# A decoder step on one core: half of the recurrence's tables on VectorE, and the sampled scores spread for two sequences at once

## The chip, the core and the metric

The kernel runs on one core of a Trainium2 chip, as one program. The metric is the device time of one execution in microseconds (us); less is better. TensorE (PE) multiplies matrices, VectorE (DVE) and GpSimd (POOL) work elementwise, ScalarE (ACT) copies and evaluates functions, and SyncE (SP) issues every DMA of this kernel, one after another. Each engine executes its own instructions in the order in which they stand in its queue.

## The reference, cut to what matters

One layer of a hybrid decoder for a prompt of 1024 rows and for 8 sequences of 8 new rows (64 sampled rows). One input projection gives queries, keys, values and the input u of a state-space group.

```
z = rmsnorm(x) @ w_in                      # 1088 rows, 1024 -> 2048 columns: q, k, v, u
# window attention, three dilations (1, 4, 16), for prompt and sample
scores = einsum(q, k) / 8 ;  p = softmax ;  out = p @ v
# S5 recurrence: h[t] = a*h[t-1] + B u[t] ;  y[t] = Re(C h[t]) + D u[t]    (complex, 32 groups x 64 states)
y = x + concat(norm(attn), norm(ssm)) @ w_out ;  y = y + (silu(y@w_gate) * (y@w_up)) @ w_down
```

For the sample, each query meets a cache of 2048 past keys per sequence: every 16th key of the far part (96 per query row), every 4th of the middle part, and all of the last 128. The recurrence is computed in blocks of 8 time steps: an input table (B times the powers of a, per group) takes 8 inputs to a state, and an output table (C times the powers of a) takes a state to 8 outputs.

## The kernel before

The program has three stages, and the change lies in the first.

**Stage A (the input projection, to about 315 us of the span).** TensorE computes 16 column pieces of `w_in` by 1088 rows; pieces 0 to 3 are q, 4 to 7 are k, 8 to 11 are u, 12 to 15 are v. Every number is split into two parts, so each product is three matmuls (lines 70, 71, 72). A piece needs its weights split: `ws`, high part by ScalarE (line 64), low part by VectorE (line 65). A k piece is copied out by ScalarE (`kr`, `kh`) and by VectorE (`kl`, line 65), and only then is its PSUM bank free for the piece three further on. Banks of tag `sd` serve the work beside the projection.

Two generators run beside the projection, and `merge` decides by their yielded weights which one writes its next instructions; a scheduler then orders each engine's queue by a timeline of its own.

- `ssm_setup` and `ssm_units`: a long chain of small VectorE instructions (`pw`, `wph`, then `D1`/`D2`, the input factors), then for 8 units `products(u)` on GpSimd: the input table `vt` (lines 574 to 576 from `D1`, `D2`) and the output table `WO` (the same three lines from `E1`, `E2`), both 128x512. `vt` and `WO` have two buffers each. `turn(u)` transposes `vt` on TensorE, `shift(q)` multiplies by `shf`, and `tables()` makes the rotation table `CP` on VectorE (lines 618 to 620). The results go to DRAM.
- `sample_scores`: 24 steps, three for each sequence. A step loads far keys `kf` and middle keys `kk`, multiplies them with the queries `qb` (`kf` on GpSimd, line 679; `kk` on VectorE, line 680), and sums over 64 columns (`Sm`, line 687; `Sf`, line 689 by VectorE or line 694 by ScalarE). After two sequences, `rest(g)` spreads the sums against selection matrices (`Z`, line 722; `Y`, line 725) and TensorE gathers them with 12 small matmuls (`sel,Z` and `sel,Y`, line 75).

**Stage B (315 to 660 us)**: prompt attention, the recurrence itself and the sampled values; it starts with loads of the stored queries and keys (`QS`, `KH`, `KL`). **Stage C (from 660 us)**: output projection and FFN.

Of the kernel before, what the change touches and what calls it, by code (L numbers as in the profile page):

```python
# [46 lines left out]
class K:  # L47
# [506 lines left out]
    def ssm_units(self, wk):  # L554
# [6 lines left out]
        def products(u):  # L561
            gs = slice(4 * u, 4 * u + 4)

            def pwb(z):
                return z[:, :, gs].rearrange("p k g -> p g k").unsqueeze(2).to_broadcast(shp)

            def mb(m):
                return m[:, gs].unsqueeze(3).to_broadcast(shp)
            wo = wk.tile([128, 4, 128], F32, tag="WO", name="WO", bufs=2)
            vt[u] = wk.tile([128, 4, 16, 8], F32, tag="vt", name="vt", bufs=2)  # L570
            ca = wo.rearrange("p g (c d) -> p g c d", c=16)
            for o, m1, m2, z in ((vt[u], D1, D2, pwr), (ca, E1, E2, pw[:, :, 1:9])):
                o2 = wk.tile([128, 4, 16, 8], F32, tag="v2", name="v2", bufs=1)
                G.tensor_tensor(out=o, in0=mb(m1), in1=pwb(z[:, 0]), op=OP.mult)
                G.tensor_tensor(out=o2, in0=mb(m2), in1=pwb(z[:, 1]), op=OP.mult)
                G.tensor_tensor(out=o, in0=o, in1=o2, op=OP.add)
            self.store(self.dWO[u], wo)

        def turn(u):
# [12 lines left out]
            V.tensor_copy(k, p[:, 0:64].rearrange("p (g c) -> p g c", c=16))  # L592
            V.tensor_tensor(k, k, dd[:, 4 * u:4 * u + 4], op=OP.add)
# [54 lines left out]
    def sample_scores(self, sp, sq):  # L648
# [3 lines left out]
        kf, kk, qb, kn, kt, Sf, Sm = ({} for _ in range(7))  # L652
        sel = sp.tile([128, 68], F32, name="sel")
        self.load(sel, I["c_sel"])
        tsel, asel, bsel, xsel = sel[:, 0:8], sel[:, 12:28], sel[:, 28:60], sel[:, 60:68]


        def loads(i):
# [15 lines left out]
            kk[i] = sq.tile([128, 3, 512], F32, tag="kk", name="kk", bufs=KKB)  # L674
            self.load(kk[i][:, 0], ck[b, 1536 + 128 * u:1664 + 128 * u])

        def products(i):
            b, u = divmod(i, 3)
            nc.gpsimd.tensor_tensor(out=kf[i], in0=kf[i], in1=qb[b][:, 0:1].to_broadcast((128, 2, 512)), op=OP.mult)  # L679
            V.tensor_tensor(out=kk[i][:, 1:3], in0=kk[i][:, 0:1].to_broadcast((128, 2, 512)), in1=qb[b], op=OP.mult)  # L680

        def reduce(i):
            b, u = divmod(i, 3)
            if u == 0:
                Sf[b] = sp.tile([128, 6, 8], F32, tag="Sf", name="Sf", bufs=3)
                Sm[b] = sp.tile([128, 3, 2, 8], F32, tag="Sm", name="Sm", bufs=3)
            V.tensor_reduce(Sm[b][:, u], kk[i][:, 1:3].rearrange("p j (h e) -> p j h e", e=64), axis=AX.X, op=OP.add)
# [30 lines left out]
        def rest(g):  # L718
            Z = sp.tile([128, 6, 2, 8, 8], F32, tag="Z", name="Z", bufs=1)
            Y = sp.tile([128, 2, 3, 2, 8, 8], F32, tag="Y", name="Y", bufs=1)  # L720
            for a in range(2):
                V.tensor_tensor(Z[:, :, a], Sf[2 * g + a].unsqueeze(3).to_broadcast((128, 6, 8, 8)),
                                tsel.unsqueeze(1).unsqueeze(1).to_broadcast((128, 6, 8, 8)), op=OP.mult)
                for v in range(2):
                    V.tensor_tensor(Y[:, v, :, a], Sm[2 * g + a][:, :, v].unsqueeze(3).to_broadcast((128, 3, 8, 8)),
                                    (tsel, xsel)[v].unsqueeze(1).unsqueeze(1).to_broadcast((128, 3, 8, 8)), op=OP.mult)
            p = self.bank("sd")
            for j in range(6):
                self.mm1(p[:, 16 * j:16 * j + 16], Z[:, j].rearrange("p a h t -> p (a h t)"), asel)
            for j in range(3):  # L730
                for v in range(2):
                    self.mm1(p[:, 96 + 32 * j:128 + 32 * j], Y[:, v, j].rearrange("p a h t -> p (a h t)"), bsel, v == 0, v == 1)
            nc.scalar.activation(self.S[:, g, 0:192], p[:, 0:192], AF.Copy)

        nc.gpsimd.memset(self.S[:, :, 320:384], 0.0)
        loads(0)
        for i in range(25):
            b, u = divmod(i, 3)
            loads(i + 1)
            if i < 24:  # L740
# [7 lines left out]
            elif u == 1 and b % 2 == 0 and b > 0:  # L748
                rest(b // 2 - 1)
            yield 4.2  # L750
        self.scores_end = (lambda: near(7), lambda: rest(3))


    def sample_values(self, sp):
# [31 lines left out]
        def soft3(g):  # L786
# [6 lines left out]
                            sel[:, 8:12].unsqueeze(1).to_broadcast((128, 96, 4)), op=OP.mult)  # L793
# [1169 lines left out]
def consts():  # L1963
# [21 lines left out]
    for b in range(8):  # L1985
# [7 lines left out]
    d["c_sel"] = np.concatenate([r[:, None] % 8 == np.arange(8), r[:, None] % 4 == np.arange(4),  # L1993
                                 r[:, None] // 8 == np.arange(16), r[:, None] // 4 == np.arange(32), (r[:, None] + 4) % 8 == np.arange(8)], axis=1).astype(np.float32)
# [27 lines left out]
```

## Time and profile before

| | |
|---|---|
| median of 3 runs | 1549.76 us (1548.33 to 1554.3) |
| the profiled execution, its own time | 1551.42 us |
| span in the profile | 1549.3 us |
| busy PE, DVE, ACT, POOL | 94%, 70%, 46%, 48% of the span |
| mean granted TensorE clock | 0.933 of full speed |

The shares are averages over the three stages. In stage C TensorE is nearly always busy; the places where TensorE stands idle or at half its clock lie in stages A and B. The rows further down are therefore taken from stretches of stage A.

### The profile page before, as it was taken

The page shows a single profiled execution, that of the slowest core. Times are in us where ns is not written, and L with a number is a line of the kernel's source. Part 1 is how long each engine was busy: PE and PEld are TensorE (multiplying, and loading weights), DVE is VectorE, ACT ScalarE, POOL GpSimd, SP SyncE. Part 2 cuts the span into 40 slices and gives each one's busy share as a digit, 9 for nine tenths or more (in the row PEclk, how much of TensorE's full clock was granted, in tenths as well). Part 3 has the DMA queues.
Part 4 walks back from the last instruction along what each step waited for, and adds up shares of the span by engine and source line. Part 5 has one row for each costly group of instructions (what it writes and reads, how often), then busy time and mean ns, then how long its engine had stood idle before and what let it go on. Part 6 is the DMA issues. An engine that isn't in the chain of part 4 may idle for free.

```text
span 1549.3 us, 28207 instructions
## 1 busy us (share of the span) xinstructions
PE 1449.9 (94%) x10005; PEld 1350.3 (87%) x10005; DVE 1078.1 (70%) x2226; ACT 716.6 (46%) x1815; POOL 744.5 (48%) x719
## 2 busy tenths in 40 slices
PE   6988988989899999899987999999999989999996
PEld 5988978867777667699987999999999989999996
DVE  7895399858856677687989555555555577579554
ACT  6233444345467667665453333333322364466443
POOL 3059545436735454411147678788775421114331
PEclk9998988958769999889998999999999999999998
DMA  9438887797775863443342266566564368689874
GB/s 222 159 115 295 246 243 231 220 240 185 198 184 159 202 168 89 141 147 119 109 127 82 92 205 217 180 198 206 176 205 135 107 252 297 191 297 329 234 233 127
DMA packets 244187, 292.90 MB, mean 189 GB/s; under 512 B 29870, under 2 KB 185358, under 8 KB 244046
## 3 DMA queue, kind: packets, MB, share of 16 engines
q1 hardware_dynamic: 244046, 291.10, 62.8%
q8 instruction: 79, 1.29, 0.4%
q14 instruction: 62, 0.51, 0.1%
HBM read 211.69 MB, written 79.35 MB: 188 GB/s over the span
## 4 chain that ended last, share of the span: by engine, by line
PE 67%; DVE 14%; DMA 8%; issue 4%; POOL 3%; ACT 2%; SPq 2%; POOLq 0%; DVEq 0%; ACTq 0%
PE pmm L70 16%; PE pmm L72 16%; PE pmm L71 16%; PE psd L75 7%; PE pmm L75 3%; PE ptr L79 2%; PE ppo L75 2%; DMA kk<-in_cache_attn_k_dram 1%; SPq L82 1%; DVE ws L65 1%; POOL P L1176 1%; PE ptr L75 1%; DMA hs<-dH 1%; DVE kk L680 1%; DMA wr<-in_w_in_dram 1%
## 5 line engine op out<-in xcount | busy, mean ns | idle before, releaser
L70 PE MATMUL pmm<-hn,ws 128*128 128x272 f32 x1232 | 358.9, 291 | 9.7 <-DVE u L1750 4.4
L72 PE MATMUL pmm<-hn,ws 128*128 128x272 f32 x1232 | 357.4, 291 | 1.9 <-DVE ws L65 1.9
L71 PE MATMUL pmm<-hn,ws 128*128 128x272 f32 x1232 | 356.4, 290 | 1.0 <-DVE hn L65 1.0
L64 ACT ACTIVATE ws<-wr 128x512 fp32r<-128x512 f32 (+2 forms) x238 | 151.6, 644 | 206.1 <-PE pmm L72 192.2
L70 PEld LDWEIGHTS pmm<-hn,ws 128*128 128x128 f32 x1232 | 233.5, 190 | 11.5 <-DVE u L1750 4.7
L72 PEld LDWEIGHTS pmm<-hn,ws 128*128 128x128 f32 x1232 | 233.1, 189 | 2.5 <-DVE ws L65 2.3
L71 PEld LDWEIGHTS pmm<-hn,ws 128*128 128x128 f32 x1232 | 233.4, 190 | 1.7 <-DVE hn L65 1.6
L65 DVE TENSOR_TENSOR ws<-wr,ws 128x512 fp32r<-128x512 f32 (+2 forms) x238 | 200.4, 848 | 48.1 <-ACT ws L64 46.7
L70 PE MATMUL pmm<-hs,ws 128*128 128x272 f32 x448 | 131.3, 294 | 5.0 <-ACT hs L64 5.0
L72 PE MATMUL pmm<-hs,ws 128*128 128x272 f32 x448 | 131.0, 295 | 0.4 <-DVE ws L65 0.4
L71 PE MATMUL pmm<-hs,ws 128*128 128x272 f32 x448 | 131.1, 293 | 0.0
L1754 POOL TENSOR_TENSOR hid<-hid,s 128x272 f32<-128x272 f32 x88 | 82.3, 941 | 55.6 <-DVE hid L1747 55.6
L65 DVE TENSOR_TENSOR ws<-st,ws 128x512 fp32r<-128x512 f32 x72 | 61.1, 850 | 59.2 <-ACT ws L64 59.2
L826 POOL TENSOR_TENSOR vs<-vr,vs 128x512 fp32r<-128x512 f32 x40 | 56.2, 1410 | 94.6 <-ACT vs L824 82.0
L679 POOL TENSOR_TENSOR kf<-kf,qb 128x1024 f32<-128x1024 f32 x24 | 63.9, 2672 | 63.2 <-DMA kf<-in_cache_attn_k_dram 30.8
L70 PEld LDWEIGHTS pmm<-hs,ws 128*128 128x128 f32 x448 | 85.8, 192 | 5.2 <-ACT hs L64 5.2
L72 PEld LDWEIGHTS pmm<-hs,ws 128*128 128x128 f32 x448 | 85.3, 191 | 0.8 <-DVE ws L65 0.7
L71 PEld LDWEIGHTS pmm<-hs,ws 128*128 128x128 f32 x448 | 85.9, 192 | 0.0
L1123 DVE CUSTOM_DVE_ANT_0 P<-pmm,lnc 128x256 f32<-128x256 f32 (+1 forms) x128 | 47.6, 377 | 54.8 <-PE pmm L75 43.4
L64 ACT ACTIVATE ws<-st 128x512 fp32r<-128x512 f32 x72 | 45.2, 628 | 80.7 <-PE pmm L72 69.3
L70 PE MATMUL pmm<-mT,ws 128*128 128x272 f32 x256 | 75.6, 300 | 0.0
L71 PE MATMUL pmm<-mT,ws 128*128 128x272 f32 x256 | 75.5, 298 | 0.0
(441 smaller groups left out, 4106.0 us busy)
## 6 DMA issues: line engine op xcount, KB each, us to landing
vr<-in_cache_attn_v_dram SPq DMA_DIRECT2D x80, 256.0 KB
wr<-dS SPq DMA_DIRECT2D x32, 512.0 KB
hs<-dH SPq DMA_DIRECT2D x28, 544.0 KB
kf<-in_cache_attn_k_dram SPq DMA_DIRECT2D x48, 256.0 KB
wr<-in_ffn_w_gate_dram SPq DMA_DIRECT2D x24, 512.0 KB
wr<-in_ffn_w_up_dram SPq DMA_DIRECT2D x24, 512.0 KB
wx<-dS SPq DMA_DIRECT2D x24, 512.0 KB
dH<-hid SPq DMA_DIRECT2D x22, 544.0 KB
```

The source lines that it names most:

```text
L64: self.nc.scalar.activation(hi, src, AF.Copy)
L65: (eng or self.nc.vector).tensor_tensor(out=lo, in0=src, in1=raw(hi), op=OP.subtract)
L70: nc.tensor.matmul(out, lhsT=wh, rhs=xh, start=start, stop=False)
L71: nc.tensor.matmul(out, lhsT=wh, rhs=xl, start=False, stop=False)
L72: nc.tensor.matmul(out, lhsT=wl, rhs=xh, start=False, stop=stop)
L75: self.nc.tensor.matmul(out, lhsT=w, rhs=x, start=start, stop=stop)
L79: self.nc.tensor.transpose(out, in_, self.ident[:n, :n])
L82: return self.nc.sync.dma_start(out=out, in_=in_).ins
L679: nc.gpsimd.tensor_tensor(out=kf[i], in0=kf[i], in1=qb[b][:, 0:1].to_broadcast((128, 2, 512)), op=OP.mult)
L826: eng.tensor_tensor(out=s[:, 1], in0=vr[i], in1=raw(s[:, 0]), op=OP.subtract)
L1123: V.tensor_tensor_reduce(out=P[h, g].rearrange("p b k -> p (b k)")[:, o:o + n], in0=s[:, o:o + n], in1=lnc[:, part, 256 - n:256], scale=-1 ...
L1754: self.mark = G.tensor_tensor(out=o, in0=o, in1=sb, op=OP.mult).ins
```

## The change: what it does

1. `products(u)`: the input table `vt` stays on GpSimd, the output table `WO` is now made by VectorE, and each has its own helper tile (`v0`, `v1`).
2. `turn(u)`: two VectorE instructions for `kr` (a copy out of PSUM, then an addition of `dd`) become one that adds while it reads PSUM.
3. `ssm_units`: the rotation table advances twice in each unit, between yields of 6.0, instead of once (four times in unit 0) between yields of 3.5.
4. `sample_scores`: the raw middle keys have their own tile `kr` with three buffers, loaded two steps ahead (`mids`), instead of a third of the tile `kk`, which was loaded one step ahead and had two buffers. `Sf` and `Sm` hold two sequences. `rest` becomes `rest1` (one `Z` and one `Y` of 128x768 each for both sequences, where 2 of 128x384 and 4 of 128x192 stood) and, one step later, `rest2` with the matmuls. A step yields 3.6 instead of 4.2. The columns of the constant `c_sel` are put in another order.

```diff
-            for o, m1, m2, z in ((vt[u], D1, D2, pwr), (ca, E1, E2, pw[:, :, 1:9])):
-                o2 = wk.tile([128, 4, 16, 8], F32, tag="v2", name="v2", bufs=1)
-                G.tensor_tensor(out=o, in0=mb(m1), in1=pwb(z[:, 0]), op=OP.mult)
...
+            for k, (eng, o, m1, m2, z) in enumerate(((G, vt[u], D1, D2, pwr), (V, ca, E1, E2, pw[:, :, 1:9]))):
+                o2 = wk.tile([128, 4, 16, 8], F32, tag=f"v{k}", name="v2", bufs=1)
+                eng.tensor_tensor(out=o, in0=mb(m1), in1=pwb(z[:, 0]), op=OP.mult)
+                eng.tensor_tensor(out=o2, in0=mb(m2), in1=pwb(z[:, 1]), op=OP.mult)
+                eng.tensor_tensor(out=o, in0=o, in1=o2, op=OP.add)
...
-            V.tensor_copy(k, p[:, 0:64].rearrange("p (g c) -> p g c", c=16))
-            V.tensor_tensor(k, k, dd[:, 4 * u:4 * u + 4], op=OP.add)
+            V.tensor_tensor(k, p[:, 0:64].rearrange("p (g c) -> p g c", c=16), dd[:, 4 * u:4 * u + 4], op=OP.add)
...
-            yield 3.5
-            for _ in range(4 if u == 0 else 1):
+            for _ in range(2):
                 next(tab, None)
-            yield 3.5
+                yield 6.0
...
+        def mids(i):
+            if i < 24:
+                b, u = divmod(i, 3)
+                kr[i] = sq.tile([128, 512], F32, tag="kr", name="kr", bufs=3)
+                self.load(kr[i], ck[b, 1536 + 128 * u:1664 + 128 * u])
...
+        def rest1(g):
+            Z[g] = sp.tile([128, 6, 128], F32, tag="Z", name="Z", bufs=1)
+            Y[g] = sp.tile([128, 2, 3, 128], F32, tag="Y", name="Y", bufs=1)
...
             loads(i + 1)
+            mids(i + 2)
...
             elif u == 1 and b % 2 == 0 and b > 0:
-                rest(b // 2 - 1)
-            yield 4.2
-        self.scores_end = (lambda: near(7), lambda: rest(3))
+                rest1(b // 2 - 1)
+            if u == 2 and b % 2 == 0 and b > 0:
+                rest2(b // 2 - 1)
+            yield 3.6
+        self.scores_end = (lambda: near(7), lambda: rest1(3), lambda: rest2(3))
```

The queues change as follows. In VectorE's queue of before, where the phases `wph` of the rotation are squared and renormalised (between the outputs `ql` of the last q piece), the chain stands by itself:

```order
L479 TENSOR_SCALAR t_672<-t_672 128x32
L480 TENSOR_TENSOR wph<-wph,t_672 128x32
L481 TENSOR_TENSOR wph<-wph,t_672 128x32
L450 TENSOR_TENSOR t_672<-wph 128x32
L451 TENSOR_TENSOR t_673<-wph 128x32
L452 TENSOR_TENSOR t_674<-wph 128x32
L453 TENSOR_TENSOR t_675<-wph 128x32
```

At the same place VectorE's queue now holds the output tables `WO` of the units between the links of that chain (`v` is their helper tile):

```order
L577 TENSOR_TENSOR WO<-WO,v_1079 128x512
L478 TENSOR_TENSOR t_672<-t_672,t_673 128x32
L575 TENSOR_TENSOR WO<-E_164,pw 128x512
L576 TENSOR_TENSOR v_1187<-E_165,pw 128x512
L479 TENSOR_SCALAR t_672<-t_672 128x32
L260 SCALAR_TENSOR_TENSOR ql<-pmm,qh 128x384
L577 TENSOR_TENSOR WO<-WO,v_1187 128x512
L480 TENSOR_TENSOR wph<-wph,t_672 128x32
L481 TENSOR_TENSOR wph<-wph,t_672 128x32
```

All 24 instructions of `WO` moved ahead of the instructions that finish `D1` and `D2`, on which GpSimd's input tables wait.

In TensorE's queue of before, the matmuls on the first `Z` stand in the middle of the last u piece (bank `ppo`), and those on `Y` 18 projection matmuls later:

```order
L72 MATMUL ppo<-xT_118,ws 128x448
L75 MATMUL psd<-sel,Z 128x16 x6
L79 MATMUL psd<-ident,kn 128x128 x4
L70 MATMUL ppo<-xT_118,ws 128x448
L71 MATMUL ppo<-xT_118,ws 128x448
```

Now they stand together, in the v pieces:

```order
L72 MATMUL pmm<-ws,xT_116 128x256
L79 MATMUL psd<-ident,kn 128x128 x4
L75 MATMUL psd<-sel,Z 128x16 x6
L75 MATMUL psd<-sel,Y 128x32 x6
L70 MATMUL ppo<-ws,xT_117 128x256
```

The first `Z` moved behind 66 more projection matmuls. The second one moved from 1008 to 1200 of the 1296 projection matmuls; the third and fourth stand behind the last one, as before.

In VectorE's queue of before, around the first `Z` and `Y`, the two halves of `Z` are apart (`QB` is another operand of TensorE, `kk`, `Sm`, `Sf` the products and sums):

```order
L680 TENSOR_TENSOR kk<-kk,qb 128x1024
L722 TENSOR_TENSOR Z<-Sf,sel 128x6x64
L687 TENSOR_REDUCE Sm<-kk 128x16
L689 TENSOR_REDUCE Sf<-kf 128x16
L680 TENSOR_TENSOR kk<-kk,qb 128x1024
L725 TENSOR_TENSOR Y<-Sm,sel 128x3x64 x2
```

Now:

```order
L693 TENSOR_REDUCE Sm<-kk 128x2x8 x2
L729 TENSOR_TENSOR Y<-Sm,sel 128x768
L684 TENSOR_TENSOR kk<-kr,qb 128x1024 x2
L693 TENSOR_REDUCE Sm<-kk 128x2x8
L695 TENSOR_REDUCE Sf<-kf 128x2x8
L693 TENSOR_REDUCE Sm<-kk 128x2x8
L695 TENSOR_REDUCE Sf<-kf 128x2x8
L713 COPY QB_101<-QR 64x4x8 x2
L727 TENSOR_TENSOR Z<-Sf,sel 128x768
```

One `Y` and one `Z` stand where six instructions stood; ahead of the `Z` there are now 9 products and 14 sums of the scores, where 6 and 9 stood.

## Rows read from the trace of the kernel before

**Rows 1.** Windows: stretch, its length, busy us (instructions) by engine, clock, DMA share, GB/s.

```profile
60.00:100.00 40.00, 40.00 (x252) 38.39 (x251) 38.97 (x163) 10.88 (x28) 13.24 (x10) 1.00 0.45 144
100.00:126.00 26.00, 14.64 (x89) 13.25 (x88) 25.83 (x25) 7.13 (x13) 21.92 (x12) 0.82 0.32 112
126.00:186.00 60.00, 60.00 (x391) 58.10 (x391) 20.48 (x26) 24.48 (x45) 40.19 (x29) 0.96 0.88 292
186.00:315.00 129.00, 111.52 (x808) 106.90 (x806) 111.81 (x104) 51.19 (x313) 63.67 (x27) 0.88 0.83 234
315.00:660.00 345.00, 324.21 (x1476) 247.15 (x1475) 246.30 (x685) 210.02 (x577) 175.96 (x245) 0.83 0.66 174
```

**Rows 2.** Windows: the three stretches of stage A at half the clock.

```profile
215.80:226.00 10.20, 6.96 (x26) 6.58 (x27) 8.64 (x12) 1.96 (x17) 4.12 (x2) 0.50 0.88 265
253.30:263.50 10.20, 6.95 (x32) 6.95 (x33) 8.60 (x11) 2.16 (x15) 5.29 (x2) 0.50 0.81 254
116.80:130.40 13.60, 7.84 (x31) 7.76 (x32) 13.57 (x10) 4.75 (x10) 13.37 (x8) 0.50 0.53 191
```

**Rows 3.** Timeline of PE: start, us, instruction [idle before it <- releaser].

```profile
115.31 0.44 PE L70 MATMUL pmm<-xT,ws 128*128 128x384 f32 x1 [3.77 <-DVE kl L65]
...
219.03 2.31 PE L75 MATMUL psd<-sel,Z 128*128 128x16 f32 x10 [5.61 <-DVE Z L722]
...
256.55 0.64 PE L75 MATMUL psd<-sel,Y 128*128 128x32 f32 x2 [4.82 <-DVE Y L725]
```

**Rows 4.** Timeline of DVE, 86 to 101 us: one form alone and beside GpSimd.

```profile
86.05 0.20 DVE L619 TENSOR_TENSOR CP<-CP,wpk 128x64 f32<-128x64 f32 x1
...
86.92 0.67 DVE L524 TENSOR_TENSOR D<-D,u 128x512 f32<-128x512 f32 x1
...
89.04 1.41 DVE L619 TENSOR_TENSOR CP<-CP,wpk 128x64 f32<-128x64 f32 x1
```

**Rows 5.** Timeline of POOL: the first input table, and one beside VectorE.

```profile
87.67 2.70 POOL L574 TENSOR_TENSOR vt<-D,pwr 128x512 f32<-128x512 f32 x2 [18.34 <-DVE D L524]
...
115.97 2.24 POOL L576 TENSOR_TENSOR vt<-vt,v 128x512 f32<-128x512 f32 x1
```

**Rows 6.** Groups by line, POOL, 60 to 180 us: count, busy us, mean ns.

```profile
L575 POOL TENSOR_TENSOR v<-E,pw 128x512 f32<-128x512 f32 x8 | 13.3, 1668 | 0.4
...
L574 POOL TENSOR_TENSOR WO<-E,pw 128x512 f32<-128x512 f32 x8 | 12.6, 1578 | 29.7 <-DVE t L479 24.3 <-DMA dWO<-WO 5.4
```

**Rows 7.** Groups by line and form, DVE, 60 to 180 us.

```profile
L593 DVE TENSOR_TENSOR kr<-kr,dd 128x64 f32<-128x64 f32 x8 | 9.3, 1158 | 0.2
...
L592 DVE COPY kr<-psd 128x64 f32<-128x64 f32 x8 | 1.7, 218 | 7.1 <-PE psd L75 7.1
```

**Rows 8.** Groups by line, DVE, 180 to 310 us.

```profile
L680 DVE TENSOR_TENSOR kk<-kk,qb 128x1024 f32<-128x1024 f32 x24 | 39.9, 1670 | 22.5 <-DMA kk<-in_cache_attn_k_dram 22.5
L687 DVE TENSOR_REDUCE Sm<-kk 128x16 f32<-128x1024 f32 x24 | 28.9, 1210 | 0.3
...
L725 DVE TENSOR_TENSOR Y<-Sm,sel 128x192 f32<-128x192 f32 x16 | 9.7, 650 | 0.0
...
L722 DVE TENSOR_TENSOR Z<-Sf,sel 128x384 f32<-128x384 f32 x8 | 4.4, 558 | 0.2
```

**Rows 9.** Timeline of DVE: first product, last spread, first instruction of prompt attention.

```profile
186.28 2.83 DVE L680 TENSOR_TENSOR kk<-kk,qb 128x1024 f32<-128x1024 f32 x1 [17.38 <-DMA kk<-in_cache_attn_k_dram]
...
307.10 1.16 DVE L725 TENSOR_TENSOR Y<-Sm,sel 128x192 f32<-128x192 f32 x4
...
315.09 0.29 DVE L1123 CUSTOM_DVE_ANT_0 P<-pmm,lnc 128x128 f32<-128x128 f32 x1 [6.83 <-PE pmm L75]
```

**Rows 10.** Chain that ended last, in order of time: start, us, what.

```profile
172.24 1.78 PE psd L75 x16
...
302.08 0.39 ACT vr L365
...
307.55 6.98 DMA KL<-dK
```

More of the change, by code (lines that the diff above doesn't have):

```diff
@@ L651, in sample_scores @@
         ck = I["cache_attn_k"][0].rearrange("b p h e -> b p (h e)")
-        kf, kk, qb, kn, kt, Sf, Sm = ({} for _ in range(7))
+        kf, kr, kk, qb, kn, kt, Sf, Sm, Z, Y = ({} for _ in range(10))
         sel = sp.tile([128, 68], F32, name="sel")
         self.load(sel, I["c_sel"])
-        tsel, asel, bsel, xsel = sel[:, 0:8], sel[:, 12:28], sel[:, 28:60], sel[:, 60:68]
+        tsel, txsel, asel, bsel = sel[:, 0:8], sel[:, 0:16].rearrange("p (v t) -> p v t", v=2), sel[:, 20:36], sel[:, 36:68]
         def loads(i):
@@ L679, in products @@
             nc.gpsimd.tensor_tensor(out=kf[i], in0=kf[i], in1=qb[b][:, 0:1].to_broadcast((128, 2, 512)), op=OP.mult)
-            V.tensor_tensor(out=kk[i][:, 1:3], in0=kk[i][:, 0:1].to_broadcast((128, 2, 512)), in1=qb[b], op=OP.mult)
+            kk[i] = sq.tile([128, 2, 512], F32, tag="kk", name="kk", bufs=KKB)
+            V.tensor_tensor(out=kk[i], in0=kr[i].unsqueeze(1).to_broadcast((128, 2, 512)), in1=qb[b], op=OP.mult)
         def reduce(i):
             b, u = divmod(i, 3)
[L684 to L687, printed above, removed]
+            g, a = divmod(b, 2)
+            if u == 0 and a == 0:
+                Sf[g] = sp.tile([128, 6, 2, 8], F32, tag="Sf", name="Sf", bufs=2)
+                Sm[g] = sp.tile([128, 2, 3, 2, 8], F32, tag="Sm", name="Sm", bufs=2)
+            V.tensor_reduce(Sm[g][:, :, u, a], kk[i].rearrange("p j (h e) -> p j h e", e=64), axis=AX.X, op=OP.add)
             if u != 1:
-                V.tensor_reduce(Sf[b][:, 2 * u:2 * u + 2], kf[i].rearrange("p j (h e) -> p j h e", e=64), axis=AX.X, op=OP.add)
+                V.tensor_reduce(Sf[g][:, 2 * u:2 * u + 2, a], kf[i].rearrange("p j (h e) -> p j h e", e=64), axis=AX.X, op=OP.add)
                 return
@@ L693, in reduce @@
                     x = kf[i][:, j, 64 * h:64 * h + 64]
-                    nc.scalar.activation(x, x, AF.Copy, accum_out=Sf[b][:, 2 + j, h:h + 1])
+                    nc.scalar.activation(x, x, AF.Copy, accum_out=Sf[g][:, 2 + j, a, h:h + 1])
         def turn(b):
@@ L792, in soft3 @@
             V.tensor_tensor(Z[:, 768:1152].rearrange("p (a t) -> p a t", t=4), S[:, g, 96:192].unsqueeze(2).to_broadcast((128, 96, 4)),
-                            sel[:, 8:12].unsqueeze(1).to_broadcast((128, 96, 4)), op=OP.mult)
+                            sel[:, 16:20].unsqueeze(1).to_broadcast((128, 96, 4)), op=OP.mult)
             for j0, n in ((0, 4), (4, 4), (8, 2)):
@@ L1991, in consts @@
     d["c_csel"] = (r[:, None] % 64 == np.arange(64)[None, :]).astype(np.float32)
-    d["c_sel"] = np.concatenate([r[:, None] % 8 == np.arange(8), r[:, None] % 4 == np.arange(4),
-                                 r[:, None] // 8 == np.arange(16), r[:, None] // 4 == np.arange(32), (r[:, None] + 4) % 8 == np.arange(8)], axis=1).astype(np.float32)
+    d["c_sel"] = np.concatenate([r[:, None] % 8 == np.arange(8), (r[:, None] + 4) % 8 == np.arange(8), r[:, None] % 4 == np.arange(4),
+                                 r[:, None] // 8 == np.arange(16), r[:, None] // 4 == np.arange(32)], axis=1).astype(np.float32)
     return d
```

24 lines of the change are left out of this document (9 added, 15 removed).

## The prediction

> **What bounds the kernel now.** I began with the windows of busy time, cut where the work changes. The changed code runs from about 60 to 310 us. From 60 to 100 us TensorE never pauses while VectorE is busy 38.97 of 40 us; from 100 to 126 TensorE works only 14.64 of 26 us and VectorE 25.83; from 126 to 186 TensorE is full again and VectorE has 40 us to spare; from 186 to 315 TensorE lacks 17.5 us and VectorE is busy 111.81 of 129 [rows 1]. So the set-up of the recurrence is held by VectorE, the middle by TensorE, and the scores by VectorE with TensorE waiting on it.
>
> TensorE's timeline names the waits to be seen in the two thin stretches: 3.77 us for `kl` at 115, 5.61 us for the first `Z`, 4.82 us for a `Y` [rows 3]. After such holes the granted clock stood at half, 1.2 GHz, three times in stage A: 116.8 to 130.4, 215.8 to 226.0 and 253.3 to 263.5 us [rows 2]. Work at half clock takes twice its time, so the loss is half the busy time there: 3.9, 3.5 and 3.5 us. Where the chain leaves stage A, it goes from the last v piece's copy at 302.08 through SP's queue to the load of `KL`, 6.98 us [rows 10], and prompt attention's first VectorE instruction comes at 315.09, 13.0 us behind that copy; VectorE's last spread had ended at 307.10 + 1.16 = 308.26 [rows 9]. TensorE's chain is thus the later one, by 6.8 us.
>
> **The change part by part.**
>
> *Output tables on VectorE.* GpSimd loses 24 instructions, three groups of 8 at 1668 to 1578 ns, about 38.5 us [rows 6]. VectorE gets 24 of 128x512. The nearest row, an addition of this size with two SBUF inputs, took 0.67 us [rows 4]: 24 x 0.67 = 16.1 us. I take that; the upper bound is GpSimd's own 1.6 us (38 us), should the powers' strided reading be slow there. In the order of VectorE's queue all 24 stand before `D1` and `D2` are finished, in the stretch where VectorE had 1 us to spare. Hence the first input table, which GpSimd began at 87.67 us behind `D` [rows 5], begins some 16 us later, near 104. Two buffers of `WO` put a wait for its store on VectorE, with `ql` and `kl` behind it; in the order 9 to 15 rows lie between a table's last addition and its buffer's next use, some 3 to 5 us, and I price the waits at 0 to 3 us.
>
> Then 24 GpSimd instructions of `vt` follow instead of 48. Alone one took 2.70 / 2 = 1.35 us, beside VectorE 2.24 [rows 5]; 24 of them are 32 to 54 us, so the last table is ready at 136 to 158, plus what the two `vt` buffers wait for TensorE. VectorE meets them with the same rotation table `CP`. A `CP` instruction of 128x64 took 0.20 us alone and 1.41 beside GpSimd [rows 4]: it ended with the GpSimd instruction. The joined `kr` should go the other way: with both inputs in SBUF the addition took 1158 ns, the copy from PSUM 218 [rows 7]; one instruction at 0.22 saves 8 x (1.158 + 0.218 - 0.22) = 9.2 us of VectorE, bounds 0 and 11.
>
> The Trainium skill, "SBUF — State Buffer", section "Who interferes with whom", says that a VectorE instruction with two SBUF inputs and a GpSimd instruction reading SBUF shut each other out for a whole instruction. The trace agrees (0.20 against 1.41). It speaks against a division of labour between these two engines: side by side, 24 + 24 would add up, 24 x 1.35 + 24 x 0.67 = 48 us. Here the order keeps `WO` out of the way, and the rule bears on `CP` alone. By it the joined `kr`, with one input in PSUM, is spared, which is the 9.2 us; without it the saving would be 8 x 0.218 = 1.7 us.
>
> For TensorE the two sides nearly balance. It gains from the projection's `kl` standing ahead of the large `CP` steps. It loses as `ws` and `kl` of the next k pieces stand among contended instructions, and as the transposes of units 0 to 6 now lie within 27 thousand projection columns, where they had been spread over 73 thousand: GpSimd, at 4 to 7 us a unit, can't keep up. I take 4 us later at the end of the k pieces, with 8 earlier and 10 later as bounds: the holes of before were at most some 11 us with 3.9 of clock.
>
> *The start of the scores.* The last `shf` matmuls, 172.24 us [rows 10], free the memory that the scores take over, and they stand in TensorE's order at nearly the same projection column as before, in a stretch without a hole. Finishing the tables sooner therefore brings nothing here. The raw keys' first load, now ahead of the queries' in SP's queue, does: the first product waited for its keys to 186.28 [rows 9]. I take 2 us (0 to 4).
>
> *Spreading for two sequences.* `Y` cost VectorE 9.7 us and `Z` 4.4 [rows 8]. Eight instructions of 768 elements, between the forms of 384 (558 ns) and 1024 (1670 ns with its share of contention), at 0.93 us are 7.4 us: 6.7 less. Three buffers of raw keys and a load two steps ahead take away the later waits for keys, 22.5 [rows 8] - 17.38 [rows 9] = 5.1 us; I count 3, since other waits take their place. VectorE then ends at 308.3 - 2 - 6.7 - 3 = 296.6, were TensorE not later.
>
> *TensorE's two holes.* The first `Z` stands 66 projection matmuls later; at 391 matmuls in 60 us [rows 1] that is 10 us. Against it, VectorE needs before it 9 products (1670), 14 sums (1210), two `ws` and four `QB` (together about 6 us), `Y` and `Z`: 15.0 + 16.9 + 6 + 1.9 = 39.8 us from the first product at about 184.3, so 224.1. TensorE, which waited from 219.03 - 5.61 = 213.4 [rows 3], would now arrive at 223.4. Of the hole about 1 us is left; with an error in it I count 2. The second `Z` stands 192 matmuls later, and VectorE has more than 10 us in hand there, so 4.82 us go. With the holes the two half-clock tails go, 3.5 + 3.5. Sum: 5.6 + 4.8 + 7.0 - 2 = 15.4 us.
>
> *Moved loads and shorter yields* change no amount of work; I price them at 0, with 3 us either way, because stores of v rows stand in SP's queue among loads that wait for VectorE.
>
> *The later stages.* The order in stage B is shuffled by some twenty places at most, with its middle unmoved; in the FFN it is the same word for word. Stage B has its own holes (324.21 busy of 345 us, clock 0.83 [rows 1]); 2% of it, 7 us either way, is what I grant to chance.
>
> **The sum.** TensorE: 302.1 + 4 - 15.4 = 290.7; plus 13.0 is 303.7. VectorE: 296.6 + 4 = 300.6, earlier, so it doesn't decide. Prompt attention begins 315.1 - 303.7 = 11.4 us sooner. The profiled execution took 1551.4, 1.7 over the median shown: 1540 against it and 1538 against the median. I say **1539 us**.
>
> **The rivals.**
>
> *The gain stops at the next late thing.* If VectorE's scores keep their 122 us from first product to last spread (contention moves from `Y` to the products) and the start slips by 4, VectorE ends at about 310, and with its own 13 us lead gone to nothing attention starts at 312 to 316: 0 to 3 us, about 1549. For it: VectorE is busy 87% there. Against: 16 small spreads less.
>
> *VectorE starves TensorE in the set-up (slower).* If an output-table instruction costs 1.4 us or more on VectorE, `D` comes 34 us later instead of 16, at about 121; 24 `vt` at 2.24 run to 175, and the last turn, shift and score loads come 14 us after today's; TensorE has its holes of 100 to 126 again behind it and half the clock. Even with 5 us won in the scores it ends near 1562. It decides from `D` ready later than about 115 us. For it: VectorE is full there. Against: 0.67 us for the nearest row.
>
> *Both thin stretches go.* If the projection also loses its 11 us of holes and 3.9 of clock, with VectorE at 296 or sooner, the time is about 1522. For it: `kl` stands sooner in the order. Against: the crowded turns.
>
> *The spread still holds TensorE* (the change doesn't do what it says): `Z` comes a hole later, nothing but the clock moves; 1548, within the first rival.
>
> **How the numbers follow.** The forecast has 0.52, its own range 1529 to 1547; the first rival 0.27 (1544 to 1556); the slower one 0.12; both stretches 0.09. A change under 0.5%, 7.7 us, can't be told from none with this kernel: faster is below 1542, slower above 1557.5. Of the forecast about 0.43 lies below 1542, with the last rival and a little of the first 0.56; slower are the second rival and stray cases of stage B, 0.13; the same 0.31. The range from 1520 to 1558 leaves out about half of the slower rival and a little of the fastest.
>
> **What would show it.** Right: no wait of 4 us or more on `sel,Z` or `sel,Y` before the last v piece; 24 `WO` instructions on VectorE near 0.6 us, over before GpSimd's first `vt` at 100 to 108; `kr` near 0.22; prompt attention's first instruction at 300 to 308. Wrong: `vt` beginning after 115, a `WO` instruction waiting for its store, the last v copy not before 298, or an attention that begins sooner and a stage B that gives it back.

## The result, and the profile after

The changed kernel takes 1563.67 us (median of 5 runs, 1560.92 to 1565.18) against 1549.76 for the kernel before beside it (5 runs, 1544.88 to 1557.53): a ratio of 1.0063, 95% interval 1.0035 to 1.0090; the two medians alone give 1.0090, the upper end of it. It is slower; 1539 had been forecast, and 1563.67 lies above the range of 1520 to 1558.

The first cut is between all that comes before the mixer's output projection (its first matmul reads `mT`) and all that comes behind it. Windows of the kernel before; columns as in rows 1:

```profile
0.00:659.57 659.57, 595.54 (x3271) 503.25 (x3271) 488.48 (x1179) 336.06 (x1032) 329.01 (x342) 0.88 0.70 194
659.57:1549.30 889.73, 854.37 (x6736) 847.03 (x6734) 589.57 (x1048) 380.58 (x784) 415.51 (x377) 0.98 0.58 185
```

Windows of the changed kernel: the same two, then those that answer to [rows 1], and the longest stretch at half the clock [rows 2]:

```profile
0.00:672.10 672.10, 601.68 (x3271) 511.63 (x3271) 498.56 (x1180) 337.48 (x1032) 289.62 (x318) 0.87 0.70 191
672.10:1562.40 890.30, 854.93 (x6736) 847.27 (x6734) 594.46 (x1047) 381.27 (x784) 407.63 (x377) 0.98 0.58 185
...
100.00:126.00 26.00, 21.76 (x118) 19.45 (x117) 25.85 (x70) 7.48 (x16) 14.09 (x9) 0.87 0.40 123
126.00:186.00 60.00, 53.03 (x358) 51.23 (x358) 27.92 (x36) 23.62 (x41) 24.50 (x16) 0.94 0.73 248
186.00:315.00 129.00, 113.27 (x787) 109.33 (x786) 106.07 (x85) 50.51 (x310) 66.29 (x27) 0.89 0.80 223
...
307.00:362.00 55.00, 45.18 (x175) 37.57 (x175) 27.27 (x78) 20.59 (x75) 10.60 (x21) 0.50 0.92 212
```

Behind the cut nothing changed (889.73 and 890.30 us, the same 6736 matmuls). Ahead of it TensorE issues the same 3271 instructions and needs 12.5 us more: its busy time is 601.68 - 595.54 = 6.1 us longer, at the lower clock (0.87 for 0.88), and its idle time is (672.10 - 601.68) - (659.57 - 595.54) = 70.4 - 64.0 = 6.4 us longer. These two numbers, idle time and busy time of one fixed set of matmuls, are what I compare from here on. Each comes from the one profiled execution of its kernel, and such executions differ by several microseconds among themselves, so a difference of a few microseconds in one of them is a hint and not a measurement.

Most of the 12.5 us arise late. TensorE's last projection matmul came at 304.5 us instead of 301.7, so 2.8 us belong to stage A and 9.7 to what follows. Up to that matmul TensorE idled 37.5 us, 1.2 less than before; behind it, up to the cut, it idled 32.9 us, 7.6 more. In the kernel before, the half clock behind the projection lasted from about 305 to 348 us (read in windows of 4 us), and here from 307 to 362.

The set-up went much as forecast. Groups of VectorE by line and form in the changed kernel, 60 to 180 us, `WO` and the joined `kr`:

```profile
L576 DVE TENSOR_TENSOR v<-E,pw 128x512 f32<-128x512 f32 x8 | 9.0, 1125 | 0.0
L575 DVE TENSOR_TENSOR WO<-E,pw 128x512 f32<-128x512 f32 x8 | 8.9, 1118 | 1.8 <-DMA dWO<-WO 1.8
L577 DVE TENSOR_TENSOR WO<-WO,v 128x512 f32<-128x512 f32 x8 | 5.6, 706 | 0.0
...
L593 DVE TENSOR_TENSOR kr<-psd,dd 128x64 f32<-128x64 f32 x8 | 1.7, 218 | 10.0 <-PE psd L75 10.0
```

Timeline of GpSimd in the changed kernel, its first input table, which answers to [rows 5]:

```profile
110.76 3.21 POOL L575 TENSOR_TENSOR vt<-D,pwr 128x512 f32<-128x512 f32 x2 [66.53 <-DVE D L524]
```

`WO` took 9.0 + 8.9 + 5.6 = 23.5 us instead of 16.1, so the tables began at 110.76 and not near 104; the recurrence's joined `kr` (line 593; two other tiles have the same name) takes 218 ns, as said [rows 7]. TensorE's thin stretch from 100 to 126 filled (21.76 us busy for 14.64), and the full one behind it thinned (53.03 for 60.00). The k pieces ended 4.5 us later (162.1 for 157.6). The scores, VectorE, 180 to 325 us, against [rows 8]:

```profile
L684 DVE TENSOR_TENSOR kk<-kr,qb 128x1024 f32<-128x1024 f32 x24 | 40.9, 1724 | 22.5 <-DMA qb<-dqs 15.7 <-DMA kr<-in_cache_attn_k_dram 6.7
...
L727 DVE TENSOR_TENSOR Z<-Sf,sel 128x768 f32<-128x768 f32 x4 | 6.0, 1508 | 3.1 <-issue 3.1
L729 DVE TENSOR_TENSOR Y<-Sm,sel 128x768 f32<-128x768 f32 x4 | 4.2, 1039 | 1.6 <-PE psd L75 1.6
```

The spread costs 6.0 + 4.2 = 10.2 us where it was 14.1, and the waits ahead of the products are 22.5 us as before, now 15.7 for queries and 6.7 for keys. Waits of TensorE in the changed kernel, 126 to 325 us (total us, times, longest):

```profile
PE psd L75 <- ACT kt L707: 7.6, 2, 4.3
PE psd L79 <- DVE kr L593: 6.4, 2, 5.8
PE psd L75 <- DVE Z L727: 3.6, 1, 3.6
PE pmm L70 <- ACT vr L365: 3.6, 3, 2.0
...
```

and two of the kernel before, 126 to 316 us:

```profile
PE pmm L70 <- ACT vr L365: 2.0, 1, 2.0
...
PE psd L75 <- ACT kt L701: 0.7, 1, 0.7
```

The two holes of [rows 3], 5.6 for `Z` and 4.8 for `Y`, have shrunk to 3.6. But `kt` stands at 7.6 where it was 0.7 and `vr` at 3.6 where it was 2.0, both copies by ScalarE, and the recurrence's `kr` has 5.8 us in one piece. Of the 7.6 us for `kt`, 3.4 lie ahead of the last projection matmul and 4.3 behind it. In stage B there is a wait that the kernel before doesn't have, for a load of the recurrence's input table (waits of TensorE in the changed kernel, 300 to 400 us):

```profile
PE psd L75 <- DMA WI<-dWI: 5.2, 1, 5.2
```

The chain out of stage A, which answers to [rows 10], shows what ScalarE was doing:

```profile
293.44 2.45 DVE Z L727
...
296.53 1.22 DVE Sf L695
...
297.77 0.55 SPq L82
...
298.36 3.48 DMA kf<-in_cache_attn_k_dram
...
302.01 2.41 POOL kf L682
...
304.44 2.71 ACT kf L700 x22
...
307.23 1.14 ACT kf L700 x9
308.37 0.54 ACT vr L365 x2
...
315.41 7.02 DMA KL<-dK
...
322.98 0.29 DVE P L1134
```

It is to be read from the bottom: attention's first VectorE instruction waits for `KL`, whose load stands in SP's queue behind the last v rows; these were copied at 308.37, behind ScalarE's sums of far keys in its queue; the sums waited for GpSimd's product, that for a far key, and its load for a buffer that VectorE's `Sf` freed, behind a `Z`. Projection's last matmul had begun four microseconds before the copy. In the kernel before, the last v piece was copied 0.4 us after its last matmul began.

### The profile page after: what moved, and what is told of

Its sections match the earlier page's. It is cut to its first block, busy times and chain, and to the rows that moved or that the text cites. A ratio compares the mean times of both kernels' runs of the same rounds, so it can differ in the third digit from the quotient of the medians.

```text
span 1562.4 us, 28167 instructions
## 1 busy us (share of the span) xinstructions
PE 1456.6 (93%) x10005; PEld 1358.9 (87%) x10005; DVE 1093.0 (70%) x2226; ACT 718.8 (46%) x1815; POOL 697.2 (45%) x695
## 4 chain that ended last, share of the span: by engine, by line
PE 70%; DVE 12%; DMA 8%; issue 4%; SPq 2%; POOL 2%; ACT 2%; POOLq 0%; DVEq 0%; ACTq 0%
PE pmm L72 17%; PE pmm L70 17%; PE pmm L71 17%; PE psd L75 7%; PE pmm L75 4%; PE ptr L79 3%; PE ppo L75 3%; SPq L82 2%; DMA kf<-in_cache_attn_k_dram 1%; DVE ws L65 1%; DMA kr<-in_cache_attn_k_dram 1%; DMA WI<-dWI 1%; DVE kk L684 1%; PE ptr L75 1%; POOL kf L682 1%
## 5 line engine op out<-in xcount | busy, mean ns | idle before, releaser
L837 POOL TENSOR_TENSOR vs<-vr,vs 128x512 fp32r<-128x512 f32 x40 | 52.7, 1320 | 100.0 <-ACT vs L835 98.4
```

What stands on the lines that cost most here:

```text
L837: eng.tensor_tensor(out=s[:, 1], in0=vr[i], in1=raw(s[:, 0]), op=OP.subtract)
```

## The experiments

Ratios are to the kernel before, run beside each. All expectations were written before the run.

**The two parts alone.** First the recurrence part alone (output tables on VectorE, joined `kr`, hand-overs of 6.0 units), then the scores part alone (merge of two sequences, raw keys in their own tile, 3.6 units).

```diff
-            yield 3.5
-            for _ in range(4 if u == 0 else 1):
+            for _ in range(2):
                 next(tab, None)
-            yield 3.5
+                yield 6.0
...
```

> The kernel before with the recurrence's part of the change alone (output tables on VectorE, joined kr, rotation table twice a unit). Theory T (the output tables cost VectorE 23.7 us instead of the 16.1 I had counted, everything behind them is late and stays late): the k pieces end 3 to 6 us later than before and the whole is 4 to 8 us slower, 1554 to 1558. Theory S (the loss comes with the scores' part): within 3 us of before, 1547 to 1553.

```diff
+            Z[g] = sp.tile([128, 6, 128], F32, tag="Z", name="Z", bufs=1)
...
-            yield 4.2
-        self.scores_end = (lambda: near(7), lambda: rest(3))
+            yield 3.6
+        self.scores_end = (lambda: near(7), lambda: rest1(3), lambda: rest2(3))
```

> The kernel before with the scores' part alone (two sequences at once, raw keys two steps ahead, shorter yields). Theory S (the loads of raw keys stand ahead of the far keys' in SP's queue, far keys come in bursts, the last of them holds the v rows' copies on ScalarE): attention starts 4 to 8 us later than before, 1554 to 1558. Theory T: the holes at sel,Z and sel,Y go and nothing is late, so 4 to 10 us faster than before, 1540 to 1546.

Measured: 1.0014 (0.9991 to 1.0037) and 1.0062 (1.0039 to 1.0085). The recurrence part stayed within theory S's 3 us; the scores part was slower by more than theory S had said. So far it looked as if the scores part carried the loss.

**The tables without the stride, and the raw keys' place in the queue**, both on the changed kernel:

```diff
-        pw = self.pw = sc.tile([128, 2, 9, 32], F32, name="pw")
+        pw = self.pw = sc.tile([128, 2, 32, 9], F32, name="pw").rearrange("p c g k -> p c k g")
```

> The changed kernel with the powers stored group by group, so that VectorE reads them with step 9 between groups and step 1 within, instead of step 32; the instructions and their count are the same. If the step is what made a multiplication 1.12 us, it drops to about 0.68, the first vt starts 6 to 8 us sooner (103 to 105). Theory T: the whole is 3 to 6 us faster than the changed kernel (1558 to 1561). Theory S: GpSimd's tables are sooner, but the scores end as late: within 2 us of 1563.7.

```diff
-        def mids(i):
-            if i < 24:
-                b, u = divmod(i, 3)
-                kr[i] = sq.tile([128, 512], F32, tag="kr", name="kr", bufs=3)
...
+            kr[i] = sq.tile([128, 512], F32, tag="kr", name="kr", bufs=3)
+            self.load(kr[i], ck[b, 1536 + 128 * u:1664 + 128 * u])
...
-            mids(i + 2)
```

> The changed kernel with the raw keys loaded one step ahead, behind the far keys of the same step, as before (still three buffers of their own). Theory S: the far keys no longer wait behind raw keys in SP's queue, the last far product ends 4 to 8 us sooner than 307 and the whole is 3 to 8 us faster than the changed kernel (1556 to 1561). Theory T: no change, 1561 to 1566.

Measured: 1.0042 (1.0020 to 1.0064) and 1.0055 (1.0034 to 1.0075). VectorE's `WO` with the powers in neighbouring words, 60 to 180 us:

```profile
L575 DVE TENSOR_TENSOR WO<-E,pw 128x512 f32<-128x512 f32 x8 | 5.5, 687 | 1.4 <-DMA dWO<-WO 1.4
L576 DVE TENSOR_TENSOR v<-E,pw 128x512 f32<-128x512 f32 x8 | 5.4, 681 | 0.0
L577 DVE TENSOR_TENSOR WO<-WO,v 128x512 f32<-128x512 f32 x8 | 5.4, 681 | 0.0
```

5.5 + 5.4 + 5.4 = 16.3 us: the mis-sized term was the stride of 32 words. The first table then began at 105.8; the 7 us of VectorE bought some 0.2%, which the two intervals don't secure. The place of the raw keys' loads in the queue is not the cause: theory S had expected 1556 to 1561 us, and 1.0055 can't be told from 1.0063.

**The scores part taken apart, on the kernel before**: the shorter steps alone; all of the part but the shorter steps; the merge alone; the recurrence part with the strideless powers.

```diff
-            yield 4.2
+            yield 3.6
```

> The kernel before with one number changed: the scores hand over after 3.6 instead of 4.2 units in each of their 25 steps; nothing else of the change is in it. Theory P (the shorter steps pull the scores' loads and products ahead of the projection's, so that TensorE and the last copies of the v rows wait for them, and this is the loss of the scores part): the kernel before with the loss of the scores part, a ratio of 1.004 to 1.008 to before, some 1560 us, and attention's first VectorE product later than 315.1 us by 5 to 15. Theory M (the merge into two-sequence tiles with the products a step ahead of their matmuls is the loss): within 0.3% of before, 1553 us, with attention's first product at 311 to 318.

```diff
# the scores part, with
-            yield 3.6
+            yield 4.2
```

> The kernel before with the scores part of the change, but with the 4.2 units per step of before. Theory P: the loss goes, 1553 to 1556 us, ratio 0.999 to 1.002. Theory M: it stays as in the scores part alone, 1560 to 1564 us, ratio 1.004 to 1.008. Under both the raw keys still come two steps ahead in their own tiles.

```diff
+            Sf[g] = sp.tile([128, 6, 2, 8], F32, tag="Sf", name="Sf", bufs=2)
...
-                rest(b // 2 - 1)
+                rest1(b // 2 - 1)
+            if u == 2 and b % 2 == 0 and b > 0:
+                rest2(b // 2 - 1)
```

> The kernel before with only the merge: sums of two sequences in one tile of two buffers, one Z and one Y product for both, TensorE's products one step later; raw keys and 4.2 units as before. Theory M: 1560 us, ratio 1.004 to 1.008, with a wait of TensorE or of the loads that before does not have. Theory P: 1551 to 1554 us, ratio 0.997 to 1.001, since 6.7 us of VectorE's work are gone and TensorE's hole for Z (5.6 us) shrinks to under 2.

```diff
# the recurrence part, with
+        pw = self.pw = sc.tile([128, 2, 32, 9], F32, name="pw").rearrange("p c g k -> p c k g")
```

> The recurrence part of the change alone, on before's scores, with the powers stored so that the tables read them in neighbouring words. The tables' WO on VectorE should take 8 x 3 x 0.70 = 17 us instead of 23.7 and the first vt should begin near 106 instead of 111 us. If the strided reading is what the recurrence part loses (1.0014 for it alone), this one comes to 0.998 to 1.000, some 1552 us; if it is hidden, 1.001 as the part alone.

Measured: 0.9985 (0.9960 to 1.0009), 1.0087 (1.0059 to 1.0115), 1.0025 (1.0004 to 1.0047), 1.0021 (0.9998 to 1.0043). The shorter steps by themselves are free, against theory P; the version with 4.2 units lost more than theory M's 1.008, and the merge alone lies between the two theories. Without the stride the recurrence part is no faster (1.0021 for 1.0014), so VectorE's 7 us are hidden there. The trace of the shorter steps holds the most useful surprise. Windows, and the first VectorE instruction of attention:

```profile
0.00:657.65 657.65, 584.00 (x3287) 497.91 (x3288) 502.50 (x1181) 337.25 (x1037) 322.96 (x342) 0.89 0.72 195
```

```profile
330.98 0.29 DVE L1123 CUSTOM_DVE_ANT_0 P<-pmm,lnc 128x128 f32<-128x128 f32 x1 [0.76 <-PE pmm L75]
```

Attention begins 15.9 us later than before, and the stage behind it still ends 1.9 us sooner (657.65 for 659.57). So the start of attention doesn't set the end: TensorE idles 73.7 us, 9.6 more than before, and its busy time is 11.5 less, at a better clock (0.89 for 0.88), though 16 more matmuls stand ahead of the cut. This execution, 1547.81 us, was one of the fastest three of twelve; over the runs the gain of clock is smaller (below), and what the ratio secures is that the late start cost nothing. With raw keys, merge and 4.2 units the sum goes the other way:

```profile
0.00:675.53 675.53, 594.02 (x3271) 505.81 (x3271) 502.30 (x1164) 338.10 (x1032) 320.89 (x342) 0.87 0.70 189
```

There the idle time is 81.5 us, 17.5 more, at the busy time of before. Some of it is a wait of 10.7 us that neither the kernel before nor the changed one has, for the loads of a state (TensorE's timeline of the same run):

```profile
321.70 0.66 PE L79 MATMUL psd<-ident,hb 128*128 128x128 f32 x2 [6.24 <-DMA hb<-in_state_ssm_im_dram]
...
326.86 0.45 PE L79 MATMUL psd<-ident,hb 128*128 128x128 f32 x1 [4.49 <-DMA hb<-in_state_ssm_im_dram]
```

But the version with only the shorter steps has the same wait, 8.0 us, and is not slower: that a wait is new doesn't make it the loss.

**Do the pieces add up?** One closing piece fewer; the raw keys back in the product's tile; the raw keys alone on before; the recurrence part with the shorter steps.

```diff
-        self.scores_end = (lambda: near(7), lambda: rest1(3), lambda: rest2(3))
+        self.scores_end = (lambda: near(7), lambda: (rest1(3), rest2(3)))
```

> The changed kernel with the last two closing pieces of the scores joined into one, so that attention takes two of its steps among them, as before, and not three. Theory E (the third early attention step is what the merge costs: it puts products of attention in front of waits that before does not have): half of the loss goes, a ratio of 1.001 to 1.004 to before. Theory H (every piece of the change only shifts TensorE's idle stretches, and none of them carries the loss by itself): 1.005 to 1.007, as the changed kernel.

```diff
# the changed kernel
-            kk[i] = sq.tile([128, 2, 512], F32, tag="kk", name="kk", bufs=KKB)
+            kk[i] = sq.tile([128, 3, 512], F32, tag="kk", name="kk", bufs=KKB)
+            self.load(kk[i][:, 0], ck[b, 1536 + 128 * u:1664 + 128 * u])
...
```

> The changed kernel with the raw keys back in the first third of the product's tile, loaded one step ahead, as before: the recurrence part, the merge of two sequences and the shorter steps stay. Theory K (the raw keys' own three buffers take away the wait that paced SyncE's queue, and the far keys and v rows then wait for GpSimd and ScalarE: 1.0087 with them against 1.0025 without them at 4.2 units per step): the loss goes, ratio 0.999 to 1.002. If it stays at 1.005 to 1.007 the raw keys are not it.

```diff
# the kernel before
+                kr[i] = sq.tile([128, 512], F32, tag="kr", name="kr", bufs=3)
+                self.load(kr[i], ck[b, 1536 + 128 * u:1664 + 128 * u])
...
+            mids(i + 2)
```

> The kernel before with only the raw keys' own tile of three buffers, loaded two steps ahead; per-sequence products, 4.2 units, recurrence as before. Theory K: slower by itself, ratio 1.004 to 1.007. Otherwise 0.998 to 1.002, and the raw keys cost only beside the merge.

```diff
# the recurrence part, with
-            yield 4.2
+            yield 3.6
```

> The recurrence part of the change with before's scores at 3.6 units per step: the two pieces that lost nothing by themselves (1.0014 and 0.9985). If pieces add up: 0.998 to 1.002, some 1553 us. Theory H: anything between 0.996 and 1.006, since the two meet in the same stretch.

Measured: 1.0118 (1.0083 to 1.0154), 1.0055 (1.0028 to 1.0083), 1.0003 (0.9982 to 1.0023), 1.0076 (1.0052 to 1.0099). Theories E and K fall, theory H's own ranges are left by the first (1.005 to 1.007) and, by little, the last (0.996 to 1.006), and the sums fall too: recurrence part 1.0014 and shorter steps 0.9985 should make 0.9999 and make 1.0076; merge 1.0025 and raw keys 1.0003 should make 1.0028 and make 1.0087.

**What is a shift of the order worth by itself?** Seven projection pieces given back to the scores; the changed kernel with 4.2; the kernel before with 3.9 and with 4.5; then the changed kernel with 3.3 and 3.9.

```diff
-                yield 6.0
+                yield 3.5
```

> The changed kernel with 3.5 instead of 6.0 units at each of the recurrence's two hand-overs, so that the set-up ends at the projection's piece 18 as before, and not at 25; WO stays on VectorE, the scores as changed. Theory B (seven pieces moved from beside the scores to beside the recurrence are the loss): 0.999 to 1.003, with the first vt later than 110.8 us or a longer wait for it on TensorE, and the scores' waits on TensorE (kt, vr: 11.2 us in the changed kernel) back under 5. Theory H (any shift of the order costs about as much): 1.004 to 1.008, as the scores part alone (1.0062).

```diff
-            yield 3.6
+            yield 4.2
```

> The changed kernel with 4.2 instead of 3.6 units per scores' step. From the recurrence part with 4.2 (1.0014) and with 3.6 (1.0076) theory B expects 0.6% less than the changed kernel, 0.999 to 1.002; from the scores part with 4.2 (1.0087) and with 3.6 (1.0062) the opposite follows, 1.007 to 1.010. Theory H has no sign for it: 0.999 to 1.010.

```diff
-            yield 4.2
+            yield 3.9
```

> The kernel before with 3.9 units per scores' step, nothing else. Theory H: 0.3 to 0.8% away from before in either direction, though no instruction is added or taken away. Theory B: between before and its 3.6 version, 0.998 to 1.001.

```diff
-            yield 4.2
+            yield 4.5
```

> The kernel before with 4.5 units per scores' step, nothing else. Theory H: 0.3 to 0.8% away from before in either direction. Theory B: 1.000 to 1.003, since one step more of the scores is left behind the projection's pieces.

```diff
-            yield 3.6
+            yield 3.3
```

> The changed kernel with 3.3 instead of 3.6 units per scores' step. Theory H (where the scores fall among the projection decides, by as much as the whole change): anything from 0.998 to 1.012, at least 0.3% away from the changed kernel's 1.0063 in one of this run and the next. Theory T (the changed kernel's instructions cost more by themselves, wherever they fall): 1.005 to 1.008 in both.

```diff
-            yield 3.6
+            yield 3.9
```

> The changed kernel with 3.9 units per scores' step. Theory H: anything from 0.998 to 1.012. Theory T: 1.005 to 1.008, between 3.6 (1.0063) and 4.2 (1.0075).

| units per step | 3.3 | 3.6 | 3.9 | 4.2 | 4.5 |
|---|---|---|---|---|---|
| kernel before | | 0.9985 (0.9960-1.0009) | 1.0050 (1.0022-1.0078) | 1 | 1.0107 (1.0065-1.0149) |
| changed kernel | 1.0052 (1.0029-1.0075) | 1.0063 (1.0035-1.0090) | 1.0043 (1.0019-1.0067) | 1.0075 (1.0047-1.0103) | |

In the order in which the program writes its instructions, the recurrence part's longer hand-overs let 25 pieces of the projection pass before the scores begin, where it had been 18 (a piece is here 24 of the 1296 projection matmuls); giving these seven back made 1.0127 (1.0086 to 1.0167), so theory B falls, and theory H's 1.008 is passed. The upper line of the table is what theory H asked for: the kernel before, with not one instruction added or taken away, moves over 1.2% as its number goes from 3.6 to 4.5, and not in order (1.07% at 4.5 is even above theory H's 0.8%). The lower line is not: the changed kernel stays within 0.32% at its four places, none of them 0.3% from 1.0063 to the better, all of them slower than before; theory T expected that and missed 1.0043 by little.

How much of the 0.63% is the order's and how much the change's own stays open. The means over four places are 1.0036 for the kernel before and 1.0058 for the changed one, 0.2% apart; over the three numbers that both have (3.6, 3.9, 4.2) they are 1.0012 and 1.0060, 0.5% apart. The runs also hold all eight combinations of the three pieces:

| | old scores, 4.2 | old scores, 3.6 | new scores, 4.2 | new scores, 3.6 |
|---|---|---|---|---|
| recurrence as before | 1 | 0.9985 | 1.0087 | 1.0062 |
| recurrence changed | 1.0014 | 1.0076 | 1.0075 | 1.0063 |

The new scores (merge and raw keys) cost 0.87%, 0.77% and 0.61% in three of the four settings and nothing (-0.13%) in the fourth, which is the one beside the changed recurrence at 3.6; the recurrence part cost 0.91% in one setting and nothing clear in the other three. So the new scores are the piece that most often goes with a loss, but no piece has a price of its own, and each of them moves the order too.

How a place costs time can be read where no instruction changed. The kernel before with 4.5 units, its windows up to the output projection and from 322 to 400 us, then TensorE's waits from 186 to 322:

```profile
0.00:678.42 678.42, 607.96 (x3272) 517.52 (x3272) 496.60 (x1180) 339.14 (x1032) 318.29 (x342) 0.85 0.69 189
...
322.00:400.00 78.00, 68.44 (x271) 54.84 (x271) 53.73 (x165) 34.34 (x114) 36.62 (x61) 0.61 0.80 198
```

```profile
PE psd L75 <- ACT kt L701: 9.3, 3, 7.9
PE psd L75 <- DVE Z L722: 6.0, 1, 6.0
```

The same wait for ScalarE's `kt` as in the changed kernel opens; TensorE idles 70.5 us, 6.4 more than at 4.2, and its busy time is 12.4 longer: once the projection has ended, TensorE is left with small products of the scores and of attention, and the granted clock there was 0.61 (over 80 us behind the projection 0.59, in the changed kernel 0.60, in the kernel before 0.66). Over the runs the granted clock tells a part of it. The kernel before, 132 runs, had a mean clock of 0.9345, which with its two levels and the mean time makes 2 x (1 - 0.9345) x 1555 = 204 us at half speed. With 4.5 units it was 237 us, with 3.6 193; the changed kernel had 213, and the kernels with the recurrence part 203 to 230. But the scores part with 4.2 units had 204, as before, and lost 0.87%, so the clock is not the whole. Within the kernel before, whose runs took from 1541.4 to 1564.1 us, time and clock go together with a correlation of -0.63.

## Why the prediction was wrong

**The set-up: right, one term mis-sized.** `WO` was 23.5 us for 16.1, within the bounds taken (16.1 to 38). By the rule of the Trainium skill, page "SBUF — State Buffer", section "Door 1: The DMA port swizzle", full bandwidth needs at least two accesses to one line of 16 bytes; a stride of 32 words has one. The runs agree (1.12 us with the stride, 0.68 without), and the row I sized it by, an addition of neighbouring words, was the wrong neighbour. The store was waited for 1.8 us, within 0 to 3. The joined `kr`, and 4 us later at the end of the k pieces (4.5), came as said; the first product 1.6 us sooner for 2 (184.7).

**The rival with the right time had the wrong reason.** "VectorE starves TensorE in the set-up" gave 1562, but decides from `D` later than 115 us and 1.4 us an instruction; it was 110.8 and 1.12, TensorE was busier from 100 to 126, and the recurrence part alone cost 0.14%, within its error (beside the shorter steps it cost 0.91%, with TensorE as busy up to 162.9 us as without them).

**The step that failed is "TensorE's two holes".** It let 15.4 us go, 8.4 of holes and 7.0 of half clock, took the last v copy's distance to attention, 13.0 us, as fixed, and subtracted both from the end. From the end of the k pieces to the projection's last matmul TensorE took 304.5 - 162.1 = 142.4 us instead of 301.7 - 157.6 = 144.1: 1.7 us were won where 15.4 were counted. The v copy then came 3.9 us behind that matmul instead of 0.4, and attention 14.6 us behind the copy instead of 13.0. So attention began at 322.98 and not at 303.7: 19.3 of the 24.5 us by which the profiled execution (1564.5) missed the 1540 that the sum gave against the profile. The rest of stage B took 4.6 us more, within the 7 that were granted. TensorE's windows over the scores, before and then after:

```profile
188.30:259.10 70.80, 59.92 (x417) 57.20 (x416) 66.34 (x59) 31.87 (x193) 38.30 (x15) 0.89 0.86 245
259.10:301.70 42.60, 40.56 (x329) 39.98 (x329) 38.73 (x35) 17.08 (x114) 23.34 (x12) 0.95 0.75 221
...
191.90:251.90 60.00, 53.46 (x372) 51.12 (x369) 58.82 (x44) 24.50 (x140) 30.91 (x11) 0.94 0.91 247
251.90:304.50 52.60, 47.66 (x352) 46.83 (x353) 41.66 (x36) 19.52 (x134) 30.54 (x12) 0.87 0.76 217
```

Idle time fell from 12.9 to 11.5 us, and the time at half clock, worked out as above, stayed near 20 us (19.8 and 20.9). Of the holes for `Z` and `Y` 6.8 us did go (10.4 to 3.6), but TensorE met the next instruction that wasn't ready, a `kt` or `vr` copy, and the half clock moved with the holes. What I did not ask is who is next to be late at each place where TensorE no longer waits. VectorE was still busy 106.07 of 129 us, and ScalarE had 128 far-key sums in its queue, one every 0.24 us, and waited for GpSimd's products ahead of them; it had the same in the kernel before. Groups of ScalarE from 180 to 325 us, after and before:

```profile
L700 ACT ACTIVATE kf<-kf 128x64 f32<-128x64 f32 x128 | 30.8, 242 | 36.0 <-POOL kf L682 36.0
...
L694 ACT ACTIVATE kf<-kf 128x64 f32<-128x64 f32 x128 | 30.8, 243 | 41.9 <-POOL kf L679 41.9
```

I had written "VectorE: 296.6 + 4 = 300.6, earlier, so it doesn't decide": its last `Sm` ended at 298.9, in fact, but its last spread ended at 319.2, since the last `Z` and `Y` stood behind TensorE's products, and attention's `P` behind them. The first rival, "The gain stops at the next late thing", had this mechanism, but took VectorE for the late one and gave 1549. VectorE's timeline:

```profile
293.44 3.17 DVE L727 TENSOR_TENSOR Z<-Sf,sel 128x768 f32<-128x768 f32 x1
...
312.21 0.36 DVE L713 COPY QB<-QR 64x32 f32<-64x32 f32 x2 [3.79 <-PE psd L75]
315.69 0.96 DVE L727 TENSOR_TENSOR Z<-Sf,sel 128x768 f32<-128x768 f32 x1 [3.11 <-issue]
318.21 0.96 DVE L729 TENSOR_TENSOR Y<-Sm,sel 128x768 f32<-128x768 f32 x1 [1.57 <-PE psd L75]
322.98 0.29 DVE L1134 CUSTOM_DVE_ANT_0 P<-pmm,lnc 128x128 f32<-128x128 f32 x1 [3.81 <-PE pmm L75]
```

**"Moved loads and shorter yields" at 0, 3 us either way, was far too narrow.** They change no amount of work, and the number alone is worth from -2 to +17 us on the kernel before. The change moved the number by six tenths, priced at 0; three tenths upward cost the kernel before more than the whole change did.

**The chance of slower was 0.13.** A sum of savings says little on a stretch in which five engines wait for one another in turn; the trace before showed that in rows I had quoted (VectorE 87% busy, TensorE 86%, clock at half three times).

**What stays open.** Which wait of the 12.5 us would have to go for the changed kernel to win, and how much of the loss is the change's own: no experiment takes a single wait away and leaves the order as it is. Moving ScalarE's sums of far keys out of the way of the last `vr` and `kt` copies was not tried, nor was holding the order of stage B. No version measured beats the kernel before; the nearest is its own with 3.6 units, 0.9985 (0.9960 to 1.0009), which can't be told from no change.

## What to carry to other kernels

Where engines take turns, don't subtract a hole: for each wait you remove, name the next instruction in that queue and who makes its input, and count the gain only up to there. Before you credit a change that also moves the order, move the order alone (one pacing number, two values); what that does to the time is the noise floor of the argument, and here it was larger than the change. Compare idle time and busy time of a fixed set of matmuls rather than a landmark such as the start of the next stage, which moved by 16 us here without cost, and keep in mind that a trace is one execution.

## What the runs showed of the hardware

A VectorE product of 128x512 fp32 with one input read at a stride of 32 words took 1.12 us, with neighbouring words 0.68. Of the eight VectorE products of 128x768, six took 0.94 to 0.96 us; the other two lay where GpSimd's products ran without a pause and took 1.31 us (at 214.90, GpSimd from 213.03 to 221.79) and 3.17 us (at 293.44, GpSimd from 290.07 to 298.85). And the granted clock was not the same from run to run of one kernel: among twelve runs of the 3.6 version of before it was 0.943 in one of 1548.7 us and 0.928 in one of 1563.5.
